# New duration estimates in the planner that places background steps among dense products

## The chip, the cores and the metric

The kernel runs on one NeuronCore of a Trainium2 chip. The metric is the device time of one execution in microseconds; three runs of the kernel before gave 1542.03, 1544.28 and 1546.81 us, median 1544.28 us. The engines: TensorE (PE in the profile, with its weight loads as PEld), VectorE (DVE), ScalarE (ACT), GpSimd (POOL), and SyncE (SP), which here only issues DMAs.

## The reference, cut to what matters

Two layers work on 256 latent tokens and 256 context tokens of width 2048. What follows is the reference shortened; norms, splits and the parameter list are left out.

```
for l in range(2):
    sh, sc, gt = split(silu(c) @ ada_w[l] + ada_b[l])            # adaLN: 2048 x 6144 weights a layer
    h, hc = x * (1 + sc) + sh, xc * (1 + scc) + shc              # the same with c_ctx for the context
    if l == 0:
        qa, ka, va, ga, ub, gb = split(h @ w_in)                 # 2048 x 6144
        ya = neighbourhood_attention(qa, ka, va, context...)     # 8 heads
        yb = s5_bidirectional(ub, ...)                           # 64 groups, states of 64, both directions
        zb = gelu(yb); zb = zb * sigmoid(zb @ glu_w + glu_b)
        y = concat([ya * silu(ga), zb * silu(gb)]) @ w_out
    else:
        q, k, v, g = split(h @ w_in)                             # 2048 x 5120
        y = (gqa_attention(rope(rms(q)), rope(rms(k)), v) * silu(g)) @ w_out
    x = layer_norm(DN_ALPHA * x + gt * y)                        # and xc after layer 0
```

## The kernel before, in words

**Dense products.** Every large product is computed to fp32 accuracy: both factors are split into a high and a low part of type fp32r, and `mm3` issues three matmuls, high by high, high by low, low by high. The kernel has 7488 dense matmuls. They come in two forms: `aform` has 128 output columns on the partitions and 512 tokens on the free axis (512 columns to stream); `bform` has 128 tokens on the partitions and 256 output columns (256 to stream). Weights come through `Stream` in pieces of 1024 words a partition (512 KB, some of 384 KB): SP loads `raw`, ScalarE makes `hi`, VectorE makes `lo`; four `raw`, four `hi` and three `lo` buffers turn round. `big_h` and `big_l` are the two parts of the modulated stream h.

**Background work.** Everything that is not a dense product (adaLN vectors, the S5 branch, attention heads, norms, RMS and rotary) is written as Python generators that run while the program is built. A generator issues some instructions, then yields. `pump()` is called after every 3 matmuls of `aform` and after every 12 of `bform`; it looks through the generators in hand and lets each whose due time has come issue its next step. So the order of all instructions on each engine is settled at build time, and the due times settle it. `force()` issues a generator's steps regardless, up to a point that what follows builds on.

**The planner.** `Clock` keeps for each engine the time at which it would be through with what was issued to it. `Clock.engine` starts an instruction when its engine is free and what it reads and overwrites is ready, and adds the instruction's cost; what it writes counts as ready a latency `lat` later. `Clock.now()` is TensorE's time. `due()` gives a step's due time: when what the generator issued last will be ready, plus `pace["margin"]` (0.3 to 0.8 us by stage), or, for steps that mostly occupy VectorE, VectorE's time less `pace["lead"]` (1 to 3 us). `Clock.dma` shares 360 GB/s among all transfers and adds 2.0 us for those issued by SP. `Clock.array` doubles the cost on TensorE after a tick in which it had little to do. The costs of all instructions are set in one place, the function `call` in the class `Timed` (L199 on), through which every instruction is issued. That is why the profile shows L212 for all of them, and groups are told apart by tiles.

**The stages that matter here.** At the start the adaLN weights of layer 0's shift and scale come as 32 pieces `adp` of 1 MB, each as two DMAs, three pieces ahead. Each piece is multiplied by a burst of small tiled matmuls `a<-adp,cst`; block by block the result becomes a part of h, and dense products run on the parts that are there. S5 parameters (`nat`, 512 KB each, turned by `sb<-ident,nat`) come in between. A matmul of plain fp32 operands is one in the program and two in the trace: a burst of 8 shows there as x16. Then S5's drive works in 16 batches: VectorE makes `dd` with six multiplications, TensorE turns it (`b<-ident,dd`), ScalarE copies it to `dT`, TensorE multiplies by `ub`. Then come scan and output of S5 (`sx` goes out to DRAM as `Sd` and back), the eight attention heads, GLU and output projection, the norm (`t`), and layer 1. The four other thirds of adaLN weights ("quads", pieces `aw`, 32 of 512 KB each) are spread over four later stages.

Of the kernel before, what the change touches and what calls it, by code (L numbers as in the profile page):

```python
# [23 lines left out]
F32 = mybir.dt.float32  # L24
# [6 lines left out]
P = 128  # L31
D = 2048
T = 256            # latent tokens, and as many context tokens
NT = 512           # tokens in all: context first, then latents
# [7 lines left out]
G = 64             # S5 groups  # L42
GH = 32            # groups in one half
Q = 8              # time steps in one S5 chunk
NC_ = NT // Q      # chunks
# [8 lines left out]
class Clock:  # L54
    """Estimates of when each engine is through with what was issued to it, for the order of issue: engines run
    what they are given in order, an instruction waits for those that wrote what it reads and for those that
    read or wrote what it writes."""
# [3 lines left out]
    def __init__(self):  # L61
        self.t = {"pe": 0.0, "dve": 0.0, "act": 0.0, "sp": 0.0, "gp": 0.0}
        self.wr, self.rd, self.slots = {}, {}, {}
        self.ready = self.floor = 0.0
        self.used, self.cols = {}, {}
        self.log = []
# [46 lines left out]
    def array(self, t, cost, rows):  # L113
        """TensorE's clock is half as fast in a tick that follows one in which it had little to do."""
# [15 lines left out]
    def dma(self, q, words, descr, outs, ins):  # L130
# [5 lines left out]
        while left > 0:                                       # room in buckets of 2 us  # L136
# [10 lines left out]
    def slot(self, pool, name, bufs, tile):  # L147
        """The tile takes the place of the one of that name bufs tiles ago."""
# [15 lines left out]
    def free(self, pool, name, bufs, n=1):  # L164
        """When n more tiles of that name have their places free."""
# [17 lines left out]
class Pool:  # L183
    """A pool whose tiles the clock knows."""
# [11 lines left out]

def _isap(x):
    return hasattr(x, "tensor") and hasattr(x, "ap")


class Timed:
    """An engine whose instructions advance the clock."""
# [4 lines left out]
    def __getattr__(self, name):  # L207
# [3 lines left out]
        def call(*a, **kw):  # L211
# [9 lines left out]
            lat = 0.06  # L221
            if kind == "pe":
                lat = 0.1
                if name == "transpose":
                    c = 0.108
                elif a[1].dtype == F32R:
                    c = 0.2162 if n > 256 else 0.1082
                elif "tile_position" in kw:
                    c = 0.05 + 0.0002 * n
                else:  # L230
                    c = 0.08 if a[1].shape[-1] <= 64 else 0.28
            elif kind == "dve":
                lat = 0.13
                two = name in ("tensor_copy", "tensor_scalar", "memset") and o.dtype != F32R
                c = 0.068 + n * (0.00056 if two else 0.00104)
                if name in ("tensor_reduce", "bn_stats"):
                    c = 0.068 + _count(a[1].shape[1:]) * 0.00104
            else:
                lat = 0.15
                c = 0.1 + n * 0.00083  # L240
# [8 lines left out]
def backbone(ctx: ExitStack, tc: tile.TileContext, A, out):  # L249
# [33 lines left out]
    def vacant():  # L283
        """Steps until the bank of hbank() is free."""
# [13 lines left out]
    # ---------------------------------------------------------------- constants  # L298
# [5 lines left out]
    negm = tabs[:, 0:64]                                     # window of the neighbourhood  # L304
# [3 lines left out]
    # small vectors as columns: 0 c, 16 c_ctx, 32 ln_g0, 48 ln_b0, 64 glu_b  # L308
# [11 lines left out]
    # silu of both conditioning vectors as stationary columns (32 wide, the rest zero)  # L320
# [10 lines left out]
    # sums over two sets of the vectors' shifts and scales  # L331
# [3 lines left out]
    mod = [const.tile([P, 2, 2, KT], F32, name=f"mod{l}") for l in range(2)]   # [shift|1+scale, c|c_ctx, kt], from the biases on  # L335

    # ---------------------------------------------------------------- streamed weights
    class Stream:
        """Pieces of weights, each at most PIECE words a partition, loaded and split ahead of their use."""
# [1608 lines left out]
```

## Time and profile before

| | |
|---|---|
| median of three runs | 1544.28 us |
| profiled execution, span from first to last instruction | 1544.0 us |
| busy: TensorE, VectorE, ScalarE, GpSimd | 1489.3, 983.3, 642.2, 153.5 us |
| moved by DMA | 332.71 MB, 215 GB/s mean |
| granted TensorE clock | 0.9 or more of full speed in nearly every fortieth of the span |

The span is the profiled execution's own time; it stands 0.3 us under the median. Busy time counts an instruction from its start to its end. Matmuls overlap in the pipeline, so what one costs is read from the distance between two starts. A row "TensorE waited for X" is idle time ended by X.

### The profile page before, as it was taken

How to read it: one execution, taken by the hardware profiler on the slowest of the kernel's cores; microseconds unless marked ns; L12 is line 12 of the kernel's file. 1: busy time of each engine (PE TensorE's matmuls, PEld its weight loads, DVE VectorE, ACT ScalarE, POOL GpSimd, SP SyncE). 2: the span in 40 equal slices, each digit the busy share in tenths (PEclk: the TensorE clock that was granted, in tenths of full speed). 3: DMA queues.
4: the chain of work that ended last, by engine and by line, in shares of the span. 5: the costliest groups of instructions: out<-in, count | busy, mean ns of one | idle time of the engine just before them, and what ended most of it. 6: DMA issues, size and time to landing. Idle time of an engine off the chain costs nothing.

```text
span 1544.0 us, 30572 instructions
## 1 busy us (share of the span) xinstructions
PE 1489.3 (96%) x12530; PEld 1276.8 (83%) x12530; DVE 983.3 (64%) x1721; ACT 642.2 (42%) x981; POOL 153.5 (10%) x308
## 2 busy tenths in 40 slices
PE   6999988999999999999999999999999999999995
PEld 3676776677699977888887899999998888999995
DVE  5356489988522787545476564866764555677587
ACT  2332334422355434434353433543543445665540
POOL 1000000000000032300000000201321111121021
PEclk9999999999999999999999999999999999999998
DMA  9999365676888686543479998665658775445684
GB/s 327 338 320 305 115 187 185 202 238 219 256 294 260 175 201 153 150 142 110 128 229 316 308 314 259 190 196 167 219 183 269 246 232 178 137 124 151 204 255 141
DMA packets 329921, 332.71 MB, mean 215 GB/s; under 512 B 40197, under 2 KB 287925, under 8 KB 329141
## 3 DMA queue, kind: packets, MB, share of 16 engines
q1 hardware_dynamic: 323540, 314.87, 65.6%
q0 software_dynamic: 6240, 15.88, 3.9%
q8 instruction: 98, 1.61, 0.4%
q14 instruction: 43, 0.34, 0.1%
HBM read 301.92 MB, written 24.54 MB: 211 GB/s over the span
## 4 chain that ended last, share of the span: by engine, by line
PE 80%; DVE 6%; DMA 5%; issue 4%; POOL 2%; SPq 1%; ACT 1%; DVEq 0%; POOLq 0%; ACTq 0%
PE m L212 60%; PE b L212 10%; PE a L212 6%; PE sb L212 4%; DVE dd L212 2%; SPq L212 1%; DVE t L212 1%; DMA aw<-in_ada_w_dram 1%; DMA gf<-in_ln_b_dram 1%; DMA nat<-in_s_c_im_dram 1%; DVE lo L212 1%; DMA adp<-in_ada_w_dram 1%; POOL gbr L212 1%; POOL rt L212 1%; DMA xs<-in_x_dram 0%
## 5 line engine op out<-in xcount | busy, mean ns | idle before, releaser
L212 ACT ACTIVATE hi<-raw 128x1024 fp32r<-128x1024 f32 (+1 forms) x253 | 265.3, 1050 | 313.6 <-PE m L212 170.8
L212 PE MATMUL m<-hi,big_h 128*128 128x256 f32 x1224 | 352.9, 288 | 1.4 <-DVE t L212 1.4
L212 PE MATMUL m<-hi,big_l 128*128 128x256 f32 x1224 | 346.2, 283 | 0.0
L212 DVE TENSOR_TENSOR lo<-raw,hi 128x1024 fp32r<-128x1024 f32 (+1 forms) x214 | 257.3, 1209 | 110.4 <-issue 56.3
L212 PE MATMUL m<-lo,big_h 128*128 128x256 f32 x1152 | 325.7, 283 | 0.0
L212 PE MATMUL m<-big_h,hi 128*128 128x512 f32 (+1 forms) x848 | 321.4, 379 | 2.1 <-DVE acc L212 1.4
L212 PE MATMUL m<-big_l,hi 128*128 128x512 f32 (+1 forms) x848 | 309.0, 364 | 0.0
L212 PE MATMUL m<-big_h,lo 128*128 128x512 f32 (+1 forms) x832 | 304.4, 366 | 0.0
L212 PEld LDWEIGHTS m<-hi,big_h 128*128 128x128 f32 x1224 | 234.2, 191 | 17.3 <-issue 16.2
L212 PEld LDWEIGHTS m<-hi,big_l 128*128 128x128 f32 x1224 | 234.3, 191 | 0.2 <-DVE big_l L212 0.2
L212 PEld LDWEIGHTS m<-lo,big_h 128*128 128x128 f32 x1152 | 220.7, 192 | 0.2
L212 PEld LDWEIGHTS m<-big_h,hi 128*128 128x128 f32 x848 | 159.9, 189 | 47.7 <-issue 20.0
L212 PEld LDWEIGHTS m<-big_h,lo 128*128 128x128 f32 x832 | 156.9, 189 | 26.6
L212 PEld LDWEIGHTS m<-big_l,hi 128*128 128x128 f32 x848 | 160.3, 189 | 20.7
L212 PE MATMUL m<-lox,big_h 128*128 128x256 f32 x384 | 108.6, 283 | 0.0
L212 PE MATMUL m<-hix,big_h 128*128 128x256 f32 x312 | 89.3, 286 | 0.0
L212 PE MATMUL m<-hix,big_l 128*128 128x256 f32 x312 | 88.2, 283 | 0.0
L212 POOL DMA_DIRECT2D Yd<-ys x64 | 37.7, 595 | 409.3 <-DVE ys L212 408.6
L212 PE MATMUL a<-aw,cst 128*32 128x256 f32 x1024 | 75.6, 388 | 2.1 <-DMA aw<-in_ada_w_dram 2.1
L212 PEld LDWEIGHTS m<-lox,big_h 128*128 128x128 f32 x384 | 73.6, 192 | 0.2
L212 ACT ACTIVATE hix<-raw 128x1024 fp32r<-128x1024 f32 x45 | 47.5, 1056 | 58.9 <-PE m L212 26.0
L212 DVE TENSOR_TENSOR lox<-raw,hi 128x1024 fp32r<-128x1024 f32 x39 | 47.7, 1222 | 25.7 <-PE m L212 11.9
(383 smaller groups left out, 2184.5 us busy)
## 6 DMA issues: line engine op xcount, KB each, us to landing
aw<-in_ada_w_dram SPq DMA_DIRECT2D x128, 512.0 KB, 5.2
raw<-in_od_w_in_dram SPq DMA_DIRECT2D x96, 512.0 KB, 3.6
raw<-in_ev_w_in_dram SPq DMA_DIRECT2D x90, 512.0 KB, 5.4
adp<-in_ada_w_dram SPq DMA_DIRECT2D x64, 512.0 KB, 7.3
raw<-in_ev_w_out_dram SPq DMA_DIRECT2D x64, 512.0 KB, 5.6
raw<-in_od_w_out_dram SPq DMA_DIRECT2D x32, 512.0 KB, 3.4
ub<-Ud SPq DMA_DIRECT2D x32, 128.0 KB, 6.2
Sd<-sx SPq DMA_DIRECT2D x16, 256.0 KB, 7.2
```

The costliest lines, as they stand in the source:

```text
L212: r = f(*a, **kw)
```

## The change

The costs in `Timed.call` are replaced; nothing else that has an effect is touched. (The diff also strips comments and docstrings, which moves every line number; L212 becomes L219.) No instruction is added or taken away: the due times change, and with them the places of the background steps on every engine.

```diff
+def _far(x):
+    step, n = next(((s, n) for s, n in reversed(x.ap[1:]) if n > 1), (1, 1))
+    return abs(step) >= 8
...
             lat = 0.06
+            far = any(_far(x) for x in [o] + ins)
             if kind == "pe":
-                lat = 0.1
+                lat = 0.17
+                tiled = "tile_position" in kw
                 if name == "transpose":
-                    c = 0.108
+                    c = 0.109
                 elif a[1].dtype == F32R:
-                    c = 0.2162 if n > 256 else 0.1082
-                elif "tile_position" in kw:
-                    c = 0.05 + 0.0002 * n
+                    c = 0.0135 + n / 2400
+                elif tiled:
+                    c = 0.0145 + 0.0004 * n
+                    if a[1].shape[0] <= 64:
+                        c *= 0.6
                 else:
-                    c = 0.08 if a[1].shape[-1] <= 64 else 0.28
+                    c = 0.06 if a[1].shape[-1] <= 64 else 0.224
+                if tiled != clock.tiled:
+                    clock.tiled = tiled
+                    c += 0.15
             elif kind == "dve":
-                lat = 0.13
-                two = name in ("tensor_copy", "tensor_scalar", "memset") and o.dtype != F32R
-                c = 0.068 + n * (0.00056 if two else 0.00104)
-                if name in ("tensor_reduce", "bn_stats"):
-                    c = 0.068 + _count(a[1].shape[1:]) * 0.00104
+                lat = 0.06
+                if name == "bn_aggr":
+                    c = 0.366
+                elif name in ("tensor_reduce", "bn_stats"):
+                    c = 0.15 + _count(a[1].shape[1:]) * 0.00104
+                elif name in ("tensor_copy", "tensor_scalar", "memset"):
+                    c = 0.15 + n * (0.00054 if o.dtype == F32R else 0.0006)
+                else:
+                    c = 0.15 + n * (0.0018 if far else 0.00104)
             else:
-                lat = 0.15
-                c = 0.1 + n * 0.00083
+                lat = 0.06
+                c = 0.2 + n * (0.0018 if far else 0.00083)
```

A dense matmul is now planned at 0.227 us (512 columns) or 0.120 us (256) where it was 0.216 or 0.108, so the planner's clock goes on faster for each product, and a step that is due after a given time comes after fewer products. A multiplication of `dd` whose operands lie 8 or more elements apart (four of the six) is planned at 1.07 us where it was 0.60, so a step that waits for VectorE comes after more products.

Three places show what moves. The first is TensorE at the end of the start stage, around its last adaLN burst (`a<-adp,cst`). Before:

```order
L212 MATMUL m<-big_h,lo_1309 128x512
L212 MATMUL sb<-ident,nat 64x64 x16
L212 MATMUL a<-adp,cst 32x256 x8
L212 MATMUL m<-big_h,hi_1263 128x512
L212 MATMUL m<-big_l,hi_1263 128x512
```

Of the changed kernel:

```order
L219 MATMUL m<-big_h,lo_1172 128x512
L219 MATMUL a<-adp,cst 32x256 x16
L219 MATMUL sb<-ident,nat 64x64 x16
L219 MATMUL m<-big_h,hi_1041 128x512
L219 MATMUL m<-big_l,hi_1041 128x512
```

The last burst stands behind 324 dense products and 96 `nat` transposes in the order before, and behind 240 and 32 now; it takes the last two pieces together, and the `nat` transposes that stood ahead of it stand right behind it.

The second is the queue of DMAs on SP, around the last two DMAs of `adp`. Before:

```order
L212 DMA adp<-in_ada_w_dram 128x4x256 x2
L212 DMA raw_1421<-in_ev_w_in_dram 128x2x512
L212 DMA nat<-in_s_c_im_dram 64x2x1024
L212 DMA adp<-in_ada_w_dram 128x4x256 x2
L212 DMA raw_1513<-in_ev_w_in_dram 128x2x512
```

Of the changed kernel:

```order
L219 DMA adp<-in_ada_w_dram 128x4x256 x2
L219 DMA raw_1249<-in_ev_w_in_dram 128x2x512
L219 DMA adp<-in_ada_w_dram 128x4x256 x2
L219 DMA nat<-in_s_c_re_dram 64x2x1024
L219 DMA raw_1321<-in_ev_w_in_dram 128x2x384
```

Ahead of the last `adp` stand 18 loads of `raw` and 4 of `nat` before, 14 and 2 now; all that SP issues up to and with it is 48.71 MB before and 45.70 MB now.

The third is TensorE in S5's drive, from the second turn of `dd` on. Before:

```order
L212 MATMUL b<-ident,dd 128x128 x8
L212 MATMUL m<-big_h,hi_1926 128x512
L212 MATMUL m<-big_l,hi_1926 128x512
L212 MATMUL m<-big_h,lo_1963 128x512
L212 MATMUL b<-ident,dd 128x128 x8
L212 MATMUL b<-ub,dT 64x64 x32
```

Of the changed kernel:

```order
L219 MATMUL b<-ident,dd 128x128 x8
L219 MATMUL m<-big_h,hi_1867 128x512
L219 MATMUL m<-big_l,hi_1867 128x512
L219 MATMUL m<-big_h,lo_1922 128x512
L219 MATMUL m<-big_h,hi_1920 128x512
L219 MATMUL m<-big_l,hi_1920 128x512
L219 MATMUL m<-big_h,lo_1963 128x512
L219 MATMUL b<-ub,dT 64x64 x16
```

Two turns of `dd` that stood 3 products apart stand 18 apart now. Over the stage, the 16 batches are spread over 198 dense products of 512 columns before (the 541st to the 738th) and over 285 now (the 544th to the 828th); the first turn still takes two batches at once.

Further on, scan and output of S5 move behind more dense products, the third adaLN quad is spread over 711 products where it was 861, the fourth over 600 where it was 732, and the adaLN matmuls come in 117 bursts where it was 123.

## Rows read from the trace of the kernel before

**Rows 1.** Page, busy time, share of the span and instructions of each engine
```profile
PE 1489.3 (96%) x12530; PEld 1276.8 (83%) x12530; DVE 983.3 (64%) x1721; ACT 642.2 (42%) x981; POOL 153.5 (10%) x308
```

**Rows 2.** Waits of TensorE: us in total, times, longest
```profile
PE b L212 <- DVE dd L212: 8.5, 8, 1.4
PE sb L212 <- DMA sx<-Sd: 3.5, 1, 3.5
PE a L212 <- DMA adp<-in_ada_w_dram: 3.1, 5, 0.9
...
PE b L212 <- DVE t L212: 2.7, 2, 1.8
...
PE b L212 <- ACT dT L212: 2.4, 1, 2.4
PE a L212 <- DMA aw<-in_ada_w_dram: 2.1, 2, 1.5
```

**Rows 3.** Stretches of the start: engines' busy us, PEclk, DMA share, GB/s
```profile
0.00:36.00 36.00, 22.02 (x150) 10.85 (x153) 19.90 (x101) 8.13 (x14) 3.97 (x12) 0.91 0.99 325
36.00:116.00 80.00, 79.72 (x575) 54.58 (x569) 37.15 (x84) 27.14 (x43) 0.00 (x0) 1.00 1.07 329
116.00:157.00 41.00, 38.72 (x377) 27.39 (x376) 24.58 (x38) 11.57 (x20) 0.00 (x0) 1.00 0.99 308
```

**Rows 4.** Timeline of TensorE at the start's end: start, duration
```profile
141.64 0.40 PE L212 MATMUL m<-big_l,hi 128*128 128x512 f32 x1
141.87 0.40 PE L212 MATMUL m<-big_h,lo 128*128 128x512 f32 x1
142.20 1.08 PE L212 MATMUL a<-adp,cst 128*32 128x256 f32 x16
143.21 0.50 PE L212 MATMUL m<-big_h,hi 128*128 128x512 f32 x1
143.54 0.40 PE L212 MATMUL m<-big_l,hi 128*128 128x512 f32 x1
...
151.44 1.15 PE L212 MATMUL sb<-ident,nat 64*64 64x64 f32 x32 [0.79 <-DMA nat<-in_s_c_im_dram]
...
154.11 1.15 PE L212 MATMUL sb<-ident,nat 64*64 64x64 f32 x32
155.19 1.07 PE L212 MATMUL a<-adp,cst 128*32 128x256 f32 x16
```

**Rows 5.** Timeline of SP's queue, the last two adaLN DMAs of the start
```profile
141.78 1.49 SPq L212 DMA_DIRECT2D adp<-in_ada_w_dram  x2
```

**Rows 6.** Critical chain, 136 to 160 us: start, us, what
```profile
140.95 10.35 DMA nat<-in_s_c_im_dram
```

**Rows 7.** VectorE on tile dd: count, duration ns min/median/max, first and last start
```profile
L212 DVE TENSOR_TENSOR dd<-bbar,pd_t x32: 1046/1072/1101, 193.9 to 305.0; 128x512 f32<-128x512 f32 x32
L212 DVE TENSOR_TENSOR dd<-dd,dt__1884 x1: 695/695/695, 196.0 to 196.0; 128x512 f32<-128x512 f32 x1
```

**Rows 8.** Stretch of the S5 drive, columns as in rows 3
```profile
197.00:310.00 113.00, 100.56 (x971) 78.17 (x970) 100.61 (x114) 46.35 (x65) 1.15 (x2) 0.98 0.64 191
```

**Rows 9.** Timeline of TensorE around the sx wait
```profile
592.65 1.98 PE L212 MATMUL sb<-sx,ee 128*64 128x64 f32 x32 [3.53 <-DMA sx<-Sd]
...
595.58 0.63 PE L212 MATMUL b<-kh,ql 128*128 128x512 f32 x1
596.01 0.63 PE L212 MATMUL b<-kh,qh 128*128 128x512 f32 x1
```

**Rows 10.** Stretches around the sx wait and of the third quad
```profile
560.00:600.00 40.00, 36.47 (x628) 28.52 (x625) 32.70 (x58) 13.89 (x38) 13.79 (x24) 0.91 0.78 185
...
806.00:880.00 74.00, 74.00 (x500) 55.73 (x499) 46.91 (x61) 30.95 (x49) 1.49 (x2) 1.00 0.90 306
880.00:960.00 80.00, 80.00 (x693) 72.37 (x692) 44.15 (x57) 28.18 (x27) 4.98 (x7) 1.00 0.92 305
```

More of the change, by code (lines that the diff above doesn't have):

```diff
@@ L65, in __init__ @@
         self.used, self.cols = {}, {}
+        self.tiled = False
         self.log = []
```

## The prediction

> **What bounds the kernel now.** First I read the page's busy times: TensorE is busy 1489.3 of 1544.0 us [rows 1], and every stage is full of dense products. The change neither adds nor removes an instruction, so the time can move only by what TensorE waits, by its clock, and by what a switch between kinds of matmul costs. Next the list of what TensorE waited for. Behind the first 36 us, which fill the pipeline and whose waits for `adp` are the 3.1 us of [rows 2], it names few things: `dd` of S5's drive 8.5 us in 8 waits, `sx` 3.5 in one, `t` of the norm 2.7, `dT` 2.4, `aw` 2.1. Then the stretches. In the start, to 157 us, the DMA engines are busy all the time (share 0.99, 1.07, 0.99) and move 325, 329 and 308 GB/s [rows 3], while TensorE is busy 79.72 of 80 us in the middle stretch: two resources are full at once, and the plan holds them in balance. In the drive, VectorE is busy 100.61 of 113 us, more than TensorE's 100.56 [rows 8]. Of the later stages, those with the third quad have DMA shares of 0.90 and 0.92 at 306 and 305 GB/s with TensorE full [rows 10].
>
> So I go through the places where the new order widens or narrows the distance between issue and use, and ask which of three has the last word there: VectorE, the DMA engines, or TensorE itself.
>
> **The drive: a gain of 7.5 us.** A batch of `dd` takes VectorE four multiplications of 1072 ns and two of about 694 ns [rows 7]: 4 x 1.072 + 2 x 0.694 = 5.68 us, and 16 batches 90.8 us. The old planner took each for 0.068 + 512 x 0.00104 = 0.60 us, 3.6 us a batch, so it asked TensorE for the result 2 us a batch too early, and that is the 8.5 us. The new costs are 1.07 and 0.68 us: 5.65 a batch. The batches are spread over 285 dense products where it was 198. Dense products of 512 columns start 0.23 us apart (141.64 and 141.87 in [rows 4]), so the 198 took 45 us of the 113 and the 285 take 65. VectorE's other work grows with the products: each 24 need one `lo`, so about four more of them; that is under 5 of the 20 us gained. Of 8.5 us I let 1.0 stay. `dT`, 2.4 us, stays: the first turn takes two batches at once in both orders, and ScalarE's copies follow in the same way.
>
> **`sx`, `t`, `aw`: gains of 3.5, 1.4 and 1.0 us.** The one wait for `sx` lasted 3.53 us, and behind it matmuls of 512 columns started 0.43 us apart (595.58 and 596.01 in [rows 9]) in place of 0.23; the granted clock of that stretch is 0.91 where it is 1.00 elsewhere [rows 10]. So the wait brought a fall of the clock with it, which cost some 2 us more. The steps from `sx` to its reading now stand 10 to 20 us of products apart where it was 7 to 13, and the scan they depend on has more room. I take 3.5 of the 5.5 us, since the wait may return in another place. The norm's first transposes of the second half come 12 products of 256 columns later, 1.4 us, of the 2.7 they waited. Of the 2.1 for `aw` I take half.
>
> **Bursts: a gain of 1.2 us.** Around a burst the distances are 0.33 us on both sides where it is 0.23 between products (141.87 to 142.20, 143.21 to 143.54 in [rows 4]). A burst thus costs 0.2 us for its switches; six fewer are 1.2 us.
>
> **The start: a loss of 10.3 us.** The last adaLN burst started at 155.19 us [rows 4]. In the new order it stands behind 84 fewer dense products and 64 fewer `nat` transposes (two rows of 1.15 us each): 84 x 0.227 + 2.3 = 21.4 us less work for TensorE, which would be there at 133.8 us. But the DMAs that have to land first are only 3.01 MB fewer, 45.70 MB. From the stretches, 36 x 0.325 + 80 x 0.329 = 38.0 MB were moved by 116 us; the other 7.7 MB at 0.308 take 25 us, so the last piece lands at 141.0 us at the earliest. From the other side: in the order before, the piece issued at 141.78 [rows 5] landed somewhere between 151.3, when the `nat` issued ahead of it had landed (140.95 + 10.35, [rows 6]), and 155.19; less 3.01 MB at 0.308, which is 9.8 us, that gives up to 145.4. I take the middle, 143.2: TensorE waits 9.4 us. Right behind the burst stand the `nat` transposes whose 512 KB are issued just behind the last piece; these land 1.7 us later at 0.308, and TensorE has nothing to cover that. The wait of 0.79 us for `nat` that ended at 151.44 [rows 4] goes: 9.4 + 1.7 - 0.8 = 10.3. The old costs held this in balance by two errors, TensorE planned 5 to 10% too fast and the DMA at 360 GB/s where it moves 308 to 329; the change corrects the first alone. The bounds: if each of the two `nat` loads costs the queue as long as the last one seems to (about 4 us), the last piece lands near 139.7 and the loss is 6; at the late end, 145.4 + 1.7 - 133.8, it is 13.3, and 2 more if the clock falls as behind `sx`.
>
> The Trainium skill, "DMA: Bandwidth & Descriptors", section "Bandwidth", speaks against this loss: it puts a limit near 358 GB/s on what HBM gives one core, and higher where the neighbour core is idle. By the page, 45.70 MB would have landed by about 128 us, an estimate, and TensorE would not wait at all. The trace differs: with its DMA engines never idle it moved 308 to 329 GB/s [rows 3].
>
> **The third quad: a loss of 2 us.** Its 32 pieces, 16.8 MB, are spread over 711 products in place of 861, some 123 us of dense work in place of 144 (products of both forms, at 0.227 and 0.120 us, counted through the order). That asks for 136 GB/s where it was 116, so 325 in place of 305: right at the level of [rows 3], where the DMA engines are full. If 308 is all that is to be had there, 17/308 of 123 us, 6.8 us, are waited; if 329, nothing. I take 2, since most of the 64 KB to 512 KB transfers beside it can slip.
>
> **The rest: a loss of 1 us.** The fourth quad is compressed likewise but beside less traffic, and in layer 1 the second head of each pair is asked for 3 to 8 us earlier. Nothing in [rows 2] shows a wait there; between 0 and 3 us, of which I take 1.
>
> **The sum.** -7.5 - 3.5 - 1.4 - 1.0 - 1.2 = -14.6; +10.3 + 2 + 1 = +13.3; together -1.3 us on the profiled execution's 1544.0, so 1542.7, and the median stands 0.3 over that: 1543 us. The gains lie between 9 and 17 us, the losses between 6 and 24.
>
> **Rival 1, faster: the start's wait stays small, 1531 us.** If the DMAs land by the time TensorE arrives (which needs 45.70 MB in 133.8 us, 342 GB/s), or if less stands in front of the last piece than the count of bytes says because `nat` is what is slow, there remain -14.6, 2 more for the clock behind `sx`, and up to +4: about 1531. For it: the 10.35 us of one `nat` [rows 6], with two of the four `nat` now moved behind. Against it: 342 GB/s is above every stretch of [rows 3].
>
> **Rival 2, slower: the DMA engines decide both in the start and in the third quad, 1554 us.** Late end in both: +13.3, +2 for a clock that falls after the wait, +6.8, +1 for the rest, less gains of 12.6 (of which `sx` is only half): about +10. It decides from the point where the last `adp` lands after 145 us. For it: shares of 0.99 to 1.07 and of 0.90 to 0.92. The Trainium skill, "TensorE: Matmul & The Clock Gate", section "HAM oscillation — how this bites in real kernels", says that gaps in TensorE's work can cost clock beyond the gap itself; the 0.91 of [rows 10] agrees.
>
> **Rival 3: the change doesn't do what it says, 1549 us.** The planner is right on the durations but VectorE is as late as before, since `lo` and `dd` share it in order; then 1 to 2 of the 8.5 us go, not 7.5, and the start's loss remains: -1.3 + 6 = about +5. Against it: 1.07 planned against 1.072 measured.
>
> **How the numbers follow.** Forecast 0.42 (1538 to 1549 by itself), rival 1 0.32, rival 2 0.17, rival 3 0.09. What can be told from no change is 0.3%, 4.6 us. Faster by more: nearly all of rival 1 and a sixth of the forecast, 0.36. Slower by more: rival 2, half of rival 3 and an eighth of the forecast with the late-end cases of the third quad, 0.28. Within: 0.36. The range goes from 1529 to 1556: it leaves out the ends where all gains come with no loss, and where all losses come in full.
>
> **What would show it.** Right: an idle time of TensorE of 8 to 12 us at 130 to 146 us, named after `adp` or `nat`, with less than 2 us for `dd` in the whole list, no `sx`, and DMA shares near 1.0 up to 145. Wrong: no wait over 3 us in the start (then rival 1), a list that still has 6 us or more for `dd` (rival 3), waits for `aw` or `raw` of over 5 us between 800 and 960 (rival 2). A granted clock below 0.95 between 130 and 160 us would add the fall of the clock to the price of the start.

## The result and the profile after

The changed kernel is slower: median 1556.77 us of 7 runs (1552.04 to 1561.52) against 1545.67 us of 7 runs of before (1542.03 to 1548.51), a ratio of 1.0072 with a 95% interval from 1.005 to 1.0093. Forecast was 1543 us, range 1529 to 1556; rival 2 (1554 us) named the right side and, with the start, one of its two places; the third quad, its other place, lost nothing. The profiled execution after has a span of 1550.5 us and took 1552.33 us, so it is one of the shorter runs. (A run's time stands 1.8 us over its span here; the forecast added 0.3.)

First what TensorE waited for after the change (us in total, times, longest), beside [rows 2]:

```profile
PE a L219 <- DMA adp<-in_ada_w_dram: 6.9, 8, 2.5
...
PE b L219 <- DVE ptl L219: 3.1, 2, 2.0
PE sb L219 <- ACT hf L219: 3.0, 1, 3.0
PE m L219 <- DVE ev L219: 3.0, 1, 3.0
...
PE b L219 <- DVE kf L219: 2.3, 3, 1.4
PE sb L219 <- DMA nat<-in_s_c_re_dram: 2.3, 1, 2.3
...
PE b L219 <- ACT dT L219: 1.9, 1, 1.9
...
PE b L219 <- DVE t L219: 1.3, 2, 0.9
...
PE a L219 <- DMA aw<-in_ada_w_dram: 0.2, 1, 0.2
```

`dd` (8.5 us) and `sx` (3.5) are gone, as forecast. But `adp` has doubled (6.9 us where it was 3.1), and `ptl`, `hf`, `ev` and more of `nat` and `kf` are new. The list alone doesn't explain a longer time, since its new rows are no longer than those that went.

The dense products come in the same order in both kernels. So I counted them along TensorE's timeline and took the time at which the same product starts in each; the differences show by stage where time was lost, whatever background work has moved. (Products are numbered from 0; the first line counts from the start of the span.)

```
span, us, between the starts of dense products       before   after   difference
     0 to   24   fill                                  37.3     44.5     +7.2
    24 to  480   start, S5 parameters                 157.3    166.7     +9.4
   480 to 1010   S5 drive                             190.2    184.0     -6.2
  1010 to 1800   gates, values, scan                  130.5    129.8     -0.7
  1800 to 2400   S5 output beside heads               201.0    201.0      0.0
  2400 to 3600   last heads, GLU, out-projection      242.7    242.1     -0.6
  3600 to 5100   norm, keys and values of layer 1     193.3    193.3      0.0
  5100 to  end   layer 1                              391.7    389.2     -2.5
```

The start lost 16.7 us where 10.3 were forecast. It lost them in three places. The first, TensorE's timeline in the fill (start, duration, instruction, idle time before and its releaser):

```profile
25.85 1.03 PE L219 MATMUL a<-adp,cst 128*32 128x256 f32 x2
27.25 2.47 PE L219 MATMUL a<-adp,cst 128*32 128x256 f32 x16 [0.37 <-DMA adp<-in_ada_w_dram]
30.28 1.06 PE L219 MATMUL a<-adp,cst 128*32 128x256 f32 x14 [0.56 <-DMA adp<-in_ada_w_dram]
33.85 1.06 PE L219 MATMUL a<-adp,cst 128*32 128x256 f32 x2 [2.51 <-DMA adp<-in_ada_w_dram]
35.34 1.93 PE L219 MATMUL a<-adp,cst 128*32 128x256 f32 x14 [0.42 <-DMA adp<-in_ada_w_dram]
```

Three pieces are asked for at once behind the third product, and TensorE waits for them; before, those pieces stood behind 6, 9 and 21 products. The second place is near 100 us, and the third the last burst:

```profile
104.04 1.15 PE L219 MATMUL sb<-ident,nat 64*128 64x64 f32 x8 [2.96 <-ACT hf L219]
...
140.40 1.48 PE L219 MATMUL a<-adp,cst 128*32 128x256 f32 x18
142.65 1.06 PE L219 MATMUL a<-adp,cst 128*32 128x256 f32 x14 [0.77 <-DMA adp<-in_ada_w_dram]
146.02 1.97 PE L219 MATMUL sb<-ident,nat 64*64 64x64 f32 x32 [2.31 <-DMA nat<-in_s_c_re_dram]
...
148.51 0.63 PE L219 MATMUL m<-big_l,hi 128*128 128x512 f32 x1
148.94 0.63 PE L219 MATMUL m<-big_h,lo 128*128 128x512 f32 x1
```

The wait at 104 us is put down to ScalarE, but ScalarE's timeline shows what it was itself waiting for:

```profile
102.02 1.06 ACT L219 ACTIVATE hi<-raw 128x1024 fp32r<-128x1024 f32 x1 [6.99 <-DMA raw<-in_ev_w_in_dram]
102.98 1.00 ACT L219 ACTIVATE hf<-sb,mod 128x256 f32<-128x256 f32 x2
```

`hi` stands ahead of `hf` in ScalarE's queue and waited 6.99 us for its DMA; `hf` reads the PSUM tile `sb` that the `nat` transposes write next. So this too is a late DMA. And behind each of the three the clock falls: the products at 148.51 and 148.94 are 0.43 us apart in place of 0.23. The stretches after (engines' busy us, PEclk, DMA share, GB/s) show the same, beside [rows 3, 8, 10]:

```profile
0.00:36.00 36.00, 19.14 (x129) 7.82 (x132) 19.89 (x101) 8.13 (x14) 3.97 (x12) 0.86 0.99 326
96.00:116.00 20.00, 17.04 (x117) 11.32 (x112) 8.64 (x36) 4.49 (x7) 0.00 (x0) 0.91 1.08 319
116.00:137.00 21.00, 20.59 (x155) 13.80 (x153) 19.22 (x32) 7.48 (x11) 0.00 (x0) 1.00 1.02 340
137.00:157.00 20.00, 16.93 (x141) 12.72 (x140) 6.35 (x11) 5.31 (x9) 0.00 (x0) 0.83 0.52 134
206.00:320.00 114.00, 108.49 (x898) 85.14 (x896) 97.13 (x112) 48.58 (x65) 2.81 (x3) 0.97 0.66 198
806.00:880.00 74.00, 74.00 (x465) 56.90 (x464) 52.24 (x69) 36.05 (x56) 1.49 (x2) 1.00 0.91 306
```

TensorE's clock is granted at 0.86, 0.91 and 0.83 in the three stretches with waits. Closer in, behind each of the three places:

```profile
33.00:39.60 6.60, 5.32 (x22) 2.68 (x23) 0.00 (x0) 0.00 (x0) 0.00 (x0) 0.50 1.08 363
104.70:107.90 3.20, 3.20 (x19) 1.73 (x22) 1.57 (x2) 0.60 (x1) 0.00 (x0) 0.50 1.09 371
145.70:152.30 6.60, 6.28 (x44) 5.47 (x45) 1.41 (x3) 1.72 (x3) 0.00 (x0) 0.50 0.03 11
```

That is the lower of the clock's two levels (1.2 in place of 2.4 GHz); the kernel before is granted 1.00 in all three, and from 29 to 213 us throughout. TensorE is busy 14.8 us in these stretches, so an estimate of what the lower level cost is half of that, 7.4 of the 16.7 us. The waits are the larger part of what is left: for `adp`, `nat` and `hf` together 12.2 us after, 3.9 before. In the drive TensorE is busy 108.49 of 114 us (100.56 of 113 before), and the third quad runs with TensorE full, as before.

### The profile page after: what moved, and what is told of

Its sections match the earlier page's. It is cut to its first block, busy times and chain, and to the rows that moved or that the text cites. A ratio compares the mean times of both kernels' runs of the same rounds, so it can differ in the third digit from the quotient of the medians.

```text
span 1550.5 us, 30587 instructions
## 1 busy us (share of the span) xinstructions
PE 1498.2 (97%) x12530; PEld 1280.6 (83%) x12530; DVE 982.6 (63%) x1721; ACT 643.1 (41%) x981; POOL 154.9 (10%) x308
## 4 chain that ended last, share of the span: by engine, by line
PE 53%; issue 4%; DVE 3%; POOL 2%; DMA 2%; ACT 1%; SPq 0%; DVEq 0%; POOLq 0%
PE m L219 41%; PE b L219 7%; PE a L219 3%; PE sb L219 2%; DVE t L219 1%; POOL rt L219 1%; DMA gf<-in_ln_b_dram 1%; POOL gbr L219 1%; DMA aw<-in_ada_w_dram 0%; POOL xp L219 0%; POOL tm L219 0%; DMA grows<-in_q_norm_g_dram 0%; ACT pr L219 0%; DMA tt<-kp 0%; DVE kf L219 0%
## 5 line engine op out<-in xcount | busy, mean ns | idle before, releaser
L219 ACT ACTIVATE hi<-raw 128x1024 fp32r<-128x1024 f32 (+1 forms) x253 | 265.4, 1051 | 295.6 <-PE m L219 180.6
L219 PE MATMUL m<-hi,big_h 128*128 128x256 f32 x1224 | 352.5, 288 | 0.3 <-DVE t L219 0.3
L219 PE MATMUL m<-hi,big_l 128*128 128x256 f32 x1224 | 346.1, 283 | 0.0
L219 DVE TENSOR_TENSOR lo<-raw,hi 128x1024 fp32r<-128x1024 f32 (+1 forms) x214 | 257.4, 1209 | 126.9 <-PE m L219 46.6
L219 PE MATMUL m<-big_h,hi 128*128 128x512 f32 (+1 forms) x848 | 323.0, 381 | 4.5 <-DVE ev L219 3.0
L219 PE MATMUL m<-lo,big_h 128*128 128x256 f32 x1152 | 325.7, 283 | 0.0
L219 PE MATMUL m<-big_l,hi 128*128 128x512 f32 (+1 forms) x848 | 310.5, 366 | 0.0
L219 PE MATMUL m<-big_h,lo 128*128 128x512 f32 (+1 forms) x832 | 305.8, 368 | 0.1
L219 PEld LDWEIGHTS m<-hi,big_h 128*128 128x128 f32 x1224 | 234.3, 191 | 15.6 <-issue 14.9
L219 PEld LDWEIGHTS m<-hi,big_l 128*128 128x128 f32 x1224 | 234.4, 191 | 0.0
L219 PEld LDWEIGHTS m<-lo,big_h 128*128 128x128 f32 x1152 | 220.6, 192 | 0.3
L219 PEld LDWEIGHTS m<-big_h,hi 128*128 128x128 f32 x848 | 160.5, 189 | 48.6 <-issue 16.3
L219 PEld LDWEIGHTS m<-big_h,lo 128*128 128x128 f32 x832 | 157.7, 190 | 27.3 <-DVE lo L219 0.5
L219 PEld LDWEIGHTS m<-big_l,hi 128*128 128x128 f32 x848 | 160.9, 190 | 20.6
L219 PE MATMUL m<-lox,big_h 128*128 128x256 f32 x384 | 108.6, 283 | 0.0
L219 PE MATMUL m<-hix,big_h 128*128 128x256 f32 x312 | 89.8, 288 | 0.0
L219 PE MATMUL m<-hix,big_l 128*128 128x256 f32 x312 | 88.2, 283 | 0.0
L219 POOL DMA_DIRECT2D Yd<-ys x64 | 37.9, 599 | 460.1 <-DVE ys L219 459.4
L219 PE MATMUL a<-aw,cst 128*32 128x256 f32 x1024 | 74.3, 388 | 0.2 <-DMA aw<-in_ada_w_dram 0.2
L219 PEld LDWEIGHTS m<-lox,big_h 128*128 128x128 f32 x384 | 73.6, 192 | 0.0
L219 ACT ACTIVATE hix<-raw 128x1024 fp32r<-128x1024 f32 x45 | 47.6, 1058 | 54.0 <-PE m L219 27.3
L219 DVE TENSOR_TENSOR lox<-raw,hi 128x1024 fp32r<-128x1024 f32 x39 | 47.6, 1221 | 27.0 <-PE m L219 20.6
```

Of the source, the lines that this page charges most:

```text
L219: r = f(*a, **kw)
```

## The experiments

Each table line gives the time of the 480th dense product (the start), the lengths of four stages, the median, and its ratio to the kernel before on the same chip. `last` is the number of dense products ahead of the last adaLN burst in the order. Times of stages are from one profiled execution of each kernel.

```
                                 last   start   480-1010  1010-1800  1800-2400  2400-3600   median   ratio (95%)
before                            324   194.5     190.2      130.5      201.0      242.7    1545.7
changed                           240   211.2     184.0      129.8      201.0      242.1    1556.8   1.0072 (1.0050 to 1.0093)
e1_pe         TensorE only        258   210.4     197.4      171.3      159.2      246.0    1573.1   1.0170 (1.0149 to 1.0191)
e2_va         others only         288   203.5     179.9      128.0      211.1      246.8    1563.1   1.0112 (1.0086 to 1.0137)
e3_start_old  old in the start    324   197.9     184.6      129.4      195.4      249.4    1541.2   0.9968 (0.9946 to 0.9989)
e4_rate       DMA at 320          294   200.0     182.9      129.7      201.3      247.5    1548.6   1.0004 (0.9990 to 1.0018)
e5_start_new  new in the start    240   209.2     194.5      139.0      196.0      242.5    1569.4   1.0166 (1.0120 to 1.0213)
e6_tiled      tiled price only    246   214.4     193.5      153.4      174.8      242.8    1569.3   1.0145 (1.0116 to 1.0174)
e7_mix        new 480 to 2700     324   194.3     186.3      128.9      195.7      244.6    1540.0   0.9962 (0.9945 to 0.9978)
e8_jit        product 1 ns less   213   214.0     183.7      128.6      196.6      244.0    1552.4   1.0043 (1.0027 to 1.0058)
e9_rate300    DMA at 300          378   199.3     183.8      130.1      200.4      241.5    1545.4   0.9987 (0.9973 to 1.0001)
e10_far       far price only      324   197.7     178.0      129.8      202.7      242.4    1536.0   0.9925 (0.9900 to 0.9949)
e11_again     changed, 2nd look   240   211.3     184.5      129.9      201.0      242.4    1555.5   (one run)
e12_heads     new to head 5       324   194.9     185.9      129.3      197.1      243.6    1537.0   0.9944 (0.9928 to 0.9960)
e13_noada     changed, less DMA   240   199.4     184.4      129.8      200.1      241.8    1545.0   0.9991 (0.9976 to 1.0007)
e14_far_mix   far, then new       324   195.3     178.8      129.8      196.6      247.1    1537.0   0.9935 (0.9912 to 0.9958)
```

The stages 1010 to 1800 and 1800 to 2400 have to be read together: where the first is long (e1, e5, e6), S5's output begins in it, at the 1500th, 1788th and 1608th product (1836th before), and the second is short.

**Which prices make the start's loss: e1_pe, e2_va, e3_start_old.** The old costs are put back beside the new ones and chosen by a flag for each kind of engine.

```diff
-            if kind == "pe":
+            if kind == "pe" and not clock.new_pe:
+                ...                                  # old costs; likewise for dve, act and gp
+            elif kind == "pe":
```

> New costs for TensorE alone, old ones for VectorE, ScalarE and GpSimd. Theory A (the start loses because the faster planner clock puts adaLN bursts behind fewer products than the DMA engines allow): the last adaLN burst stands behind 258 products (324 before, 240 changed), so the 480th dense product starts 12 to 15 us later than before's 194.5 us. The drive keeps its dd waits (7 us or more), since VectorE is planned too fast as before. In all 1555 to 1560 us. Rival B (the start's loss comes from the shorter latencies of VectorE and ScalarE, which let the steps of h be issued too early): the start is within 3 us of before, in all 1542 to 1547 us.

> New costs for VectorE, ScalarE and GpSimd alone, old ones for TensorE. Theory A: the last adaLN burst stands behind 288 products, so the start loses some 6 to 8 us against before; the drive's dd waits go (7 us less idle there); in all 1542 to 1547 us. Rival B: the whole loss of the start, 14 to 17 us, is here, and in all it is 1551 to 1557 us.

> Old costs to the end of the start stage, all new ones behind it. If the start alone makes the change slower (theory A and B alike): the 480th dense product within 1 us of before's 194.5 us, then the gains that the changed kernel has behind it, 8 to 11 us: 1533 to 1538 us. Rival C (the gains of the drive are only time that the start's delay had already given back, because adaLN and S5 parameters were through earlier against the products): then about 1541 to 1546 us.

The start lost 15.9 us with TensorE's new prices alone, 9.0 with the others alone, 3.4 with none (the same order as before; the other four kernels with it came at 194.3 to 197.7, so this is how far one order varies). The two late ones, e3 and e10, are granted 0.50 of the clock from 153.5 to 159.9 us, behind a wait for `nat` of 1.3 us; the others are granted 1.00 there, e14 too, whose wait was 1.6 us. So both halves of the change move the bursts, TensorE's more; B falls. e1's total is 13 us above the expected range: its drive took 7.2 us more than before's, with 9.4 us of waits for `dd`, and the stages from 2400 to 5100 took 8.7 us more. e2's total missed by far: a single wait of 8.8 us for `lo` beside the S5 output, and 11.6 us more behind the 2400th product.

With old costs in the start the kernel is faster than before, though less than expected. The total, 1541.2 us, lies in the range of rival C, but its reason does not hold: the gain of the drive is there (5.6 us), and what is missing went in the stage of the third quad, which lost 6.7 us, with 4.1 us of waits for `aw` in 9 places.

**The planner's DMA rate: e4_rate, e9_rate300.**

```diff
-        busy = max(words * 4 / 360e3, 0.18)
+        busy = max(words * 4 / 320e3, 0.18)         # 300e3 in e9_rate300
```

> All new costs, and the planner shares 320 GB/s in place of 360 among the DMAs, near what the start's stretches show. Theory A: the last adaLN burst moves back behind 294 products; the start loses 4 to 7 us against before in place of 16.7, later stages as in the changed kernel: 1538 to 1544 us. Rival D (the loss comes from the first burst at the fourth dense product and from falls of the clock, and not from the planner's DMA rate): the start still loses 12 us or more, 1549 to 1556 us.

> All new costs, and the planner shares 300 GB/s among the DMAs in place of 360, a little less than the start's stretches show (308 to 329). The last adaLN burst stands behind 378 products. Theory A: TensorE no longer waits for adp behind the first 40 us; the 480th dense product at 192 to 197 us; in all 1534 to 1542 us. Rival D (falls of the clock and the first bursts make the loss): 1549 us or more. Rival G (too late now: products run out of what is prepared, so TensorE waits for h): the start loses 5 us or more through waits for hf or big_h.

At 320 the start's loss fell from 16.7 to 5.5 us, as A has it; the total missed A's 1538 to 1544 us, since the stage of the third quad took 4.8 us more, and is that of before. At 300 the fill was the shortest of all (34.9 us, where before has 37.3), but the start still lost 4.8 us: A's 192 to 197 was missed by 2.3 us and its total by 3.4. The bursts now come late, as G has it, but the waits are not those that G named: 2.8 us for `acc` and 1.3 for `arow` in the start, 0.2 for `big_h`. That lateness is the reason is argued, not shown. D falls with both.

**Where the loss is put, and by which line: e5_start_new, e6_tiled, e7_mix.** e5 and e7 switch the flags at the end of the start (e7 back again behind the last head). e6 has one edit on before:

```diff
-                    c = 0.05 + 0.0002 * n
+                    c = 0.0145 + 0.0004 * n         # tiled matmuls, without the factor 0.6
+                ...                                  # and 0.15 for each switch to or from them
```

> All new costs in the start stage, old ones behind it: the reverse of the kernel with old costs in the start. Theory A (the start's loss is the start's own): the 480th dense product 14 to 18 us later than before's 194.5 us, as in the changed kernel (16.7); the drive's dd waits of 7 us or more are back; in all 1557 to 1565 us. Rival C (the stages behind give the start's delay back, since adaLN and S5 parameters are through earlier): 1545 to 1552 us.

> One line of the change: only the tiled matmuls (adaLN bursts and S5 pieces) get their new cost, with 0.15 us for each switch; all else as before. In the order this alone moves the last adaLN burst from behind 324 products to behind 246; the dense products' new cost alone moves it to 303, each of the other edits to 306 to 321. Theory A with this as its main term: the start loses 13 to 18 us against before, in all 1555 to 1563 us. Rival E (the position of the last burst does not measure the loss; the dense products' cost or the first burst's place does): under 6 us lost in the start, since the first bursts stand behind 6 and 9 products as before; in all 1545 to 1551 us.

> Old costs in the start, new ones for S5's drive, scan and the attention heads, old ones again from GLU on. Theory A with stages that add up: start as before (194 to 198), drive 6 and scan and heads 6 us shorter than before as with old costs in the start alone, GLU and output projection as before (242.5 where the kernel with new costs there took 250.2): 1530 to 1536 us. Rival F (what the later stages take depends on what the stages ahead left, so that gains of stages don't add): 1538 to 1545 us.

The new costs in the start alone lost 14.7 us there, and nothing behind gave it back; later stages even lost some, so that the total, 1569.4 us, lies above A's range. e6 lacks the change's factor 0.6 for tiled matmuls of 64 rows or fewer; the adaLN bursts have 128 rows, so this touches the stages behind the start alone. The price of the tiled matmuls alone, which in the start are the bursts, lost 19.9 us there, more than all the changes together: it is the main term, not the dense product that I had named. Its size was above A's 18 us, and so was the total (1569.3 us); E falls. e7 kept the start (194.3) and gained in drive and heads, but norm and layer 1's first products took 5.2 us more (198.5 where before has 193.3): stages don't add freely, as F has it.

**A difference that means nothing, and a second look: e8_jit, e11_again.**

```diff
-                    c = 0.0135 + n / 2400
+                    c = 0.0125 + n / 2400
```

> All new costs, but a dense product is planned 1 ns cheaper (0.226 in place of 0.227 us). A difference that means nothing by itself, yet it moves steps: the last adaLN burst stands behind 213 products where it was 240. Theory A: the start loses 18 to 23 us against before, as the position of the last burst sets it; in all 1556 to 1566 us. If the time were a draw by which steps happen to meet: the start anywhere between 195 and 215 us.

> The changed kernel itself, for a second profile: its runs lay from 1552.0 to 1561.5 us, and the profile at hand is of one of 1552.3. If the start is what makes it slower, the 480th dense product is again 14 to 20 us later than before's 194.5 us, and a longer run has its extra time in falls of the clock behind waits in the start, not in the stages behind. If a later stage has it, that stage is longer by 4 us or more than in the first profile.

One nanosecond moved the last burst to 213 products, and the start went to 214.0 us with it, as A forecast. (A draw between 195 and 215 us could have given 214.0 too; against it stands only that the start follows the burst's place over all kernels of the table.) Later stages happened to gain 4.4 us beside the heads, so the total came out below what was expected. The second profile of the changed kernel has the start at 211.3 us, within 0.1 of the first; its 3.3 us more of span lie 0.5 in the drive and 2.1 in layer 1, and not in the start as was expected. The longest runs (1559.8 to 1561.5) are in no profile.

**The drive's gain: e10_far.** One term on before:

```diff
-                c = 0.068 + n * (0.00056 if two else 0.00104)
+                c = 0.068 + n * (0.00056 if two else 0.0018 if far else 0.00104)
```

> One term of the change on the order of before: VectorE's products with operands 8 or more elements apart cost 0.068 + 0.0018 n us in the planner; all else as before. The start's order is then before's. The 16 batches of the drive stand behind 540 to 819 products, as in the changed kernel. If the planner's price of dd made the drive's waits: dd waits under 2 us in place of 8.5, the stage from the 480th to the 1010th product 5 to 8 us shorter than before's 190.2; start 194 to 198; in all 1536 to 1541 us. Rival H (other prices, as the latencies, let the waits go): dd waits of 5 us or more stay and the time is within 3 us of before.

The drive became 12.2 us shorter, more than in the changed kernel, and no wait for `dd` is left in the list, whose first rows are:

```profile
PE sb L222 <- DMA tt<-kp: 4.3, 6, 1.3
PE m L222 <- DMA brow<-in_ada_b_dram: 3.2, 1, 3.2
PE m L222 <- DMA crow<-in_c_ctx_dram: 3.0, 1, 3.0
PE b L222 <- DVE t L222: 2.7, 2, 1.8
```

This one term of the change beats both kernels: 0.75% faster than before, with an interval from 0.5% to 1.0%. H falls.

**Whether the gains add: e12_heads, e14_far_mix.**

> As the mixed kernel (old costs in the start, new in drive, scan and heads, old again behind), but the old costs return at the sixth attention head and not only behind the eighth. If the two to three us that the mixed kernel lost around the last heads (waits for ptl) came from the new prices there: 1532 to 1537 us. If they came from what the stages ahead left over (stages that don't add): 1538 to 1542 us, as the mixed kernel.

> Before's costs with the one price for far operands (which took the drive's waits away) up to the end of S5's scan, all new costs from there to the fifth attention head, before's costs with the far price behind. If stages add: start 194 to 198, drive 178, scan's output and heads 195 to 197 in place of 202.6, the rest as with the far price alone: 1527 to 1533 us. If they don't (a gain in one stage comes back as a wait in the next): 1534 to 1540 us.

e12's median is 3 us under e7's, but the intervals of the two ratios overlap, and 1537.0 lies at the border of the two expectations, so that question stays open. In the profiles it gained 1.0 us beside the last heads, where the `ptl` waits were, and 1.9 behind them, and lost 1.4 at the first heads. e14 had all three good stages at once (195.3, 178.8, 196.6) and lost 4.4 us in the next, so it ends where e10 does, as was expected if stages don't add. What a stage hands on decides some 5 us of the next.

**The DMA engines with the order held: e13_noada.**

```diff
+            if n >= 12:
+                ...                                  # counted by the planner, not issued
+                nc.gpsimd.memset(t, 0.001)
+            else:
                 for s in range(2):
                     SY.dma_start(t[:, :, s, :], ...)
```

> The changed kernel with its order on TensorE unchanged, but the adaLN pieces of layer 0 from the thirteenth on (20 of 32 MB) are not loaded; GpSimd fills their tiles with a constant, while the planner still counts them as DMAs. The adaLN values are therefore not those of the reference. Theory A (DMA landing makes the start's waits): no wait for adp or nat behind the first 45 us, the first 24 products as late as in the changed kernel (44 us), the 480th product at 195 to 201 us in place of 211.2; in all 1537 to 1545 us. Rival D (the order itself, by switches and falls of the clock): 207 us or more, in all 1548 us or more.

The order on TensorE is the changed kernel's (bursts, `dd` turns and quads stand behind the same numbers of products), but behind the twelfth piece the DMA engines have little to do. Its stretches, columns as above, and its last burst:

```profile
44.00:100.00 56.00, 55.27 (x426) 36.49 (x425) 20.81 (x38) 19.19 (x35) 23.52 (x13) 1.00 0.50 155
100.00:137.00 37.00, 35.37 (x281) 23.28 (x282) 31.18 (x69) 12.06 (x18) 13.27 (x8) 1.00 0.29 92
```

```profile
135.08 1.93 PE L222 MATMUL a<-adp,cst 128*32 128x256 f32 x32
136.94 1.15 PE L222 MATMUL sb<-ident,nat 64*64 64x64 f32 x32
```

The granted clock is 1.00 from 44 to 200 us, no wait precedes the burst or the turn of `nat` behind it, and the 480th product starts at 199.4 us, in A's range: of 16.7 us, 11.8 are gone, and the medians differ by as much (1556.8 and 1545.0, the upper end of A's range). D falls. From product 24 on, the same order takes 155.9 us where it took 166.7, and before's order 157.3. Before's order was not run with these loads taken away, but of its waits between 36 and 200 us only 0.8 us are for a DMA (`nat`, [rows 4]), so it had little to gain. So in these stages the order itself costs little or nothing; late DMAs do, with the clock that falls behind them. The fill, whose first pieces were still loaded, kept its loss: 43.4 us against 44.5.

## Why the prediction was wrong

**The start: right cause and side, mis-sized: 16.7 us for 10.3.** The landing of the last piece was forecast at 143.2 us, and the second half of its burst began at 142.65; the `nat` behind it was forecast for 144.9 and came at 146.02. The step that failed is the sum of this one term, 9.4 + 1.7 - 0.8: it has the work that moved behind the burst too small, and the fall of the clock at nothing. In its place the runs showed three late DMAs with a fall of the clock behind each, and 16.7 us. In detail:

- *The fill was left out.* I read the waits of the first 36 us as those that fill the pipeline and priced only the end of the start, though the order moved three bursts there too. It took 7.2 us more. Because of it, and of the wait near 100 us, TensorE came to the last burst at 140.4 us and not at 133.8, and so waited 3.1 us there, not the 9.4 + 1.7: the same late landing, paid for earlier. So the fill is no further term of the sum: in e1 and e6 the 24th product started at 37.7 and 37.9 us, nearly as before, and the start lost 15.9 and 19.9 us all the same. The sign that I had set failed with it: behind the fill no wait of the start is over 3 us (the longest has 2.96), which by the prediction spoke for rival 1, the faster one.
- *The work left behind the burst was short by 2.3 us.* These 64 `nat` transposes are written as plain fp32 matmuls with `ident`, and so are two each in the trace: four rows of x32, 4.6 us. I took the two rows of [rows 4]; the kernel before has two more ahead of them:

```profile
133.96 1.15 PE L212 MATMUL sb<-ident,nat 64*64 64x64 f32 x32
...
136.91 1.15 PE L212 MATMUL sb<-ident,nat 64*64 64x64 f32 x32
```

- *The clock was left to the late end.* Behind the wait at 146 us TensorE ran at the lower level (granted 0.50) to 152 us: nine products, each 0.2 us longer, and the turn of `nat` 1.97 us where it is 1.15, together 2.6 us. The Trainium skill, "TensorE: Matmul & The Clock Gate", section "HAM oscillation — how this bites in real kernels", says that gaps cost clock beyond themselves; the three stretches granted at 0.83 to 0.91 agree. I had cited it for a rival and not in the sum.

10.3 + 2.3 + 2.6 + 1.1 for the later `nat` gives 16.3 of the 16.7. This counts along the last landing, which the two earlier falls of the clock do not add to; counted by waits and clock, all three falls together are the 7.4 us estimated above.

**The reason behind it was half right.** I named the dense product's price as what unbalanced planner and DMA. e6 shows the bursts' price as the main term: alone it moves the last burst from 324 to 246 products; the dense price alone moves it to 303 in the planner's order, which was not run. Whichever moves it, the start follows: 324 products 194.3 to 197.9 us (six kernels), 294 200.0, 288 203.5, 258 210.4, 246 214.4, 240 209.2 to 211.3 (three), 213 214.0. Between 324 and 240 that is 16.7/84 = 0.20 us for each product, nearly the whole 0.23 us that one takes: while the DMA engines are full, a product that no longer stands ahead of the burst is roughly a product's time lost. It is not a strict rule: 246 lost more than 240, and as much as 213.

**The drive: right.** -7.5 was forecast and the waits of 8.5 us are gone; the stage is 6.2 us shorter in the changed kernel, 12.2 with the far price alone. Why the far price alone does better stays open.

**`sx`: right that it goes, wrong on what is left.** The wait of 3.53 us and the fall of clock behind it went, but the stage takes 201.0 us as before. The first attention heads now meet the S5 output on VectorE, and TensorE waits for `ptl`, 1.05 and 2.01 us:

```profile
648.71 0.39 PE L219 MATMUL b<-ptl,vh 128*128 128x256 f32 x1 [1.05 <-DVE ptl L219]
...
653.10 0.39 PE L219 MATMUL b<-ptl,vh 128*128 128x256 f32 x1 [2.01 <-DVE ptl L219]
```

VectorE's timeline has the S5 work (`ee`, `yt`, `ys`) ahead of `ptl` in its queue:

```profile
649.18 0.67 DVE L219 TENSOR_TENSOR ee<-cc,pe_t 128x512 f32<-128x512 f32 x1
649.78 0.67 DVE L219 TENSOR_TENSOR et<-cc,pe_t 128x512 f32<-128x512 f32 x1
650.49 0.69 DVE L219 TENSOR_TENSOR ee<-ee,et 128x512 f32<-128x512 f32 x1
651.10 0.42 DVE L219 SCALAR_TENSOR_TENSOR yt<-yt,ys 128x256 f32<-128x256 f32 x1
...
652.37 0.68 DVE L219 TENSOR_TENSOR ptl<-b,pth 128x512 fp32r<-128x512 f32 x1
```

**`t`: 1.4 us less, as forecast, and lost again:** `kf` went from 0.9 us in two waits to 2.3 in three. **Third quad: forecast +2, measured -0.6** with `aw` waits of 0.2 us. It stands on an edge: the kernels e2, e3, e4 and e14 lost 4 to 7 us in that stage. **The rest: forecast +1, measured -2.5;** no run shows why.

On the profiled pair the stages sum to +6.5 us where -1.3 were forecast: the start +6.4, `sx` +3.5, and -2 from the rest. The medians are 11 us apart, as the profiled run is one of the shorter ones. What makes the longer runs longer stays open.

## What to carry to other kernels

Estimates that are wrong on two sides can hold two full resources in balance; correcting one side alone takes the balance away, so correct the DMA model together with the engines' (here that gave no more than the time of before: ratios of 1.0004 and 0.9987), or apply only the term that mends a wait in the trace (here the price of far operands: 0.75% faster). Count a moved group in the trace's own rows, look at a reordered stage from its first instruction, the pipeline's fill too, and put the fall of the clock into the sum beside every new wait of TensorE. A sum of stages read from one profile is good to some 5 us here, since each stage hands its lateness on.

## What the runs showed of the hardware

The rate at which full DMA engines move bytes fell with one kind of transfer. In the changed kernel's trace, three stretches with the DMA engines full (columns as above):

```profile
88.00:94.50 6.50, 6.50 (x56) 4.16 (x54) 3.01 (x5) 0.88 (x3) 0.00 (x0) 1.00 1.09 350
94.50:100.00 5.50, 5.42 (x35) 3.67 (x35) 1.12 (x2) 0.53 (x2) 0.00 (x0) 1.00 1.07 198
100.00:106.00 6.00, 3.04 (x15) 2.31 (x14) 1.12 (x2) 2.56 (x4) 0.00 (x0) 0.88 1.08 338
```

A `nat` transfer, 512 KB into 64 partitions, was issued at 89.92 us, and its packets run from 94 to 100 us: there the engines move 198 GB/s at a share of 1.07, and 338 to 350 on both sides. The kernel before has the same around the packets of the `nat` issued at 140.95 us:

```profile
141.20:146.10 4.90, 4.90 (x38) 3.44 (x37) 2.40 (x4) 1.05 (x3) 0.00 (x0) 1.00 1.07 359
146.20:150.40 4.20, 4.20 (x31) 2.65 (x29) 3.45 (x5) 1.95 (x3) 0.00 (x0) 1.00 1.08 230
150.40:155.40 5.00, 4.21 (x76) 3.25 (x78) 1.37 (x2) 0.69 (x2) 0.00 (x0) 1.00 1.07 366
```

All four `nat` loads of both kernels show it: 195 to 241 GB/s at shares of 0.90 to 1.10 while their packets run. It doesn't need a queue of other loads: in e13_noada one comes behind a stretch without traffic, and the engines are nearly full at 242 GB/s:

```profile
138.30:143.30 5.00, 5.00 (x51) 3.98 (x51) 2.38 (x4) 2.15 (x4) 0.00 (x0) 1.00 0.00 0
143.40:145.80 2.40, 2.40 (x14) 2.04 (x13) 1.23 (x4) 1.03 (x3) 0.00 (x0) 1.00 0.95 242
```

Whether the 64 partitions or the rows of 4 KB make the difference was not tried. So the 308 GB/s of [rows 3] is a mixture, with two `nat` loads in it; the planner's 360 GB/s is close to what the stretches beside them move and far off for `nat`. The last piece of the start was late in part by this: 138.80 to 144.80 us, with the `nat` issued right behind it under way, moved 241 GB/s. Rival 1 was right that `nat` is what is slow, but one of them still stood where it hurt.

For what HBM gives one core the Trainium skill names a limit of about 358 GB/s ("DMA: Bandwidth & Descriptors", section "Specifications"). The planner's 360 GB/s is near it, and the 359 and 366 of the stretches above lie at it and a little over it.

A late weight load can also stop TensorE by way of an engine that neither of them names: ScalarE's queue stood 6.99 us behind one `raw`, and with it the part of h whose PSUM tile TensorE needed.
